# Later tokens' scores of both head halves in one stretch, and low weight parts in operations of 1024 columns, in the mixers of a streaming encoder step

## The chip, the cores and the metric

The kernel runs on 1 core of one Trainium2 chip. The metric is device time in microseconds: 1081.46 us is the median of 3 runs of the kernel before (1081.15 to 1081.49).

## What is computed

One inference step of a two-layer encoder, in float32, for 256 prompt tokens and 32 later tokens ("sample") that also see 512 cached keys and values. A layer is a gated feed-forward block, a mixer, and a second feed-forward block; the mixer is differential attention beside a pooling mixer and a short gated convolution. The part that the change touches is the attention, cut here to its core:

```
q, k, v, u, hc, bg, cg = split(rmsnorm(x) @ w_in)       # D_MODEL 1024 -> 2560
q = rope(q.reshape(b, t, 4, 2, 64)); k = rope(k...)     # 4 heads, 2 halves c of 64
s = einsum('bqhcd,bkhcd->bhcqk', q, k) * 64**-0.5       # later tokens: 512 cached keys + 32 new ones
p = softmax(s)                                          # over keys, for each half
a = p[:, :, 0] - lam * p[:, :, 1]
o = rmsnorm(einsum('bhqk,bkhe->bqhe', a, v), subln)     # into concat(...) @ w_out
```

## The kernel before

The 288 tokens lie along the free dimension, features along the partitions. Every large product is made from two parts of each operand, a rounded high part and the low rest: `mm3` (line 261) issues three TensorE matmuls of 288 columns, wh with xh, wl with xh, wh with xl. Weights come in chunks of 128 x 2048 floats (16 blocks of 128 x 128), loaded by DMA up to three chunks ahead. ACT rounds a chunk to wh, DVE subtracts to get wl. In the feed-forward stages this is done in operations of 1024 columns (lines 108, 109).

In the mixers the order on ACT, DVE and POOL is written by a planner inside the kernel (lines 440 to 560), and so is the place of small work between TensorE's products. Work beside the products is a set of tasks (Python generators). A task runs one step, yields `wait(...)`, and is taken up again when the planner's clock has reached the time at which it is ready: the end of its last step plus LAG = 0.2, and where it needs a PSUM bank, MARGIN = 1.1 more and a free bank. `main` (line 558) issues one triple, moves the clock by 0.369 and polls the tasks. Every step's instructions are charged to their engine with a cost from their length (an ACT copy of 288 columns from PSUM 0.29, of 512 columns from SBUF 0.53; a DVE operation 0.07 + n/960), behind what the planner has already put there. Each engine runs its instructions in the order in which they were issued. In the trace, ACT, DVE and POOL instructions of the mixers all carry line 553, the helper that charges them; they are told apart by tiles.

- `chunk` (line 580) hands out the current chunk; if its split is not complete it issues the rest first, and it starts `split_task` (line 565) for the next chunk. A chunk has two pieces of 8 blocks, a = 0 and 1, and before the change a piece is split in two halves of 4 blocks (SPLIT = 4): wh of a half on ACT, then wl of it on DVE.
- The mixer's chunks 0 to 9 hold w_in, two output tiles each (piece a is tile a, one block per k); chunks 10 to 13 hold w_out. The order of tiles is q0, k0, q1, k1, v0, v1, q2, k2, v2, v3, q3, k3 and then the gates and pools. After a tile, `after` (line 872) starts its task at once: for q and k `rope` (line 611), which begins with four ACT copies of 32 partitions into zw, then z = acc times cosR on DVE, zw times sinR on POOL, and the sum on DVE.
- `attn_p(h)` (line 657) makes the prompt's attention of a head: scores of both halves into the PSUM tile sc, mask and maximum on DVE, exponentials on ACT, transposes and value product through the two tp banks.
- `attn_s` (line 740) makes the later tokens' attention of all four heads at once, head h on partitions 32h to 32h + 31. For each half c in turn it takes sc, multiplies in two column ranges of 272 keys, takes the maximum over 544 and the exponentials. Then the halves are combined, transposed in five blocks, and multiplied with the values in one PSUM tile (line 784).
- `finish_until` (line 942) makes the products with w_out wait for what the tasks deliver; the later tokens' part ("ms") is wanted with the second of four groups.

PSUM has four accumulators, sc of two banks, and two tp banks.

```python
            def ready_at(t):
                _, res, _, dep = t[1]
                at = t[0]
                if dep is not None:
                    at = max(at, done.get(dep, never) + LAG)
                return max(at + MARGIN, min(free[res])) if res else at
```

Of the kernel before, what the change touches and what calls it, by code (L numbers as in the profile page):

```python
# [9 lines left out]
F32 = mybir.dt.float32  # L10
F32R = mybir.dt.float32r
I32 = mybir.dt.int32
AF = mybir.ActivationFunctionType
ALU = mybir.AluOpType
AX = mybir.AxisListType
# [3 lines left out]
P = 128  # L19
D = 1024  # L20
KD = D // P
SEQ = 256
DEC = 32
T = SEQ + DEC
PAST = 512
DEPTH = 2
DFF = 2816
KF = DFF // P
H = 4
HD = 64  # L30
# [34 lines left out]
def tile_step(ctx, tc, xT, head, w_gu, w_dn, w_in, w_out, rest, ck, cvp,  # L65
              yT, kT_o, vT_o, pool_o, conv_o):
    nc = tc.nc
    V, S, G, PE = nc.vector, nc.scalar, nc.gpsimd, nc.tensor

    const = ctx.enter_context(tc.tile_pool(name="const", bufs=1))  # L70
# [3 lines left out]
    tmp = ctx.enter_context(tc.tile_pool(name="tmp", bufs=2))  # L74
    ps_a = ctx.enter_context(tc.tile_pool(name="ps_a", bufs=4, space=PSUM))
    ps_s = ctx.enter_context(tc.tile_pool(name="ps_s", bufs=1, space=PSUM))
    ps_t = ctx.enter_context(tc.tile_pool(name="ps_t", bufs=2, space=PSUM))
# [197 lines left out]
    lam_s = const.tile([P, DEPTH * 2], F32, tag="lam_s", name="lam_s")  # L275

    def lambda_sums():
        lp = const.tile([P, DEPTH * 2, HD], F32, tag="lam_p", name="lam_p")
        la = lam_in.rearrange("o (a b) d -> o a b d", b=2)
        V.tensor_tensor(lp, la[:, :, 0, :], la[:, :, 1, :], ALU.mult)  # L280
        V.tensor_reduce(lam_s, lp, AX.X, ALU.add)
        for l in range(DEPTH):
            li = 0.8 - 0.6 * math.exp(-0.3 * l)
            V.tensor_scalar(gsub[:, l:l + 1], par_t[:, C_SUB + l:C_SUB + l + 1], 1.0 - li, None, ALU.mult)
# [140 lines left out]
    def mixer(l, g_next):  # L425
        with tc.tile_pool(name="mp", bufs=1) as mp, tc.tile_pool(name="mt", bufs=2) as mt, \
                tc.manual_schedule(engines={ET.Activation, ET.DVE, ET.Pool}):
            kts = mp.tile([P, H, PAST + DEC], F32, tag="kts", name="kts")
# [4 lines left out]
            qT = [mp.tile([P, T], F32, tag=f"q{h}", name=f"q{h}") for h in range(H)]  # L433
# [5 lines left out]
            es_t = mp.tile([P, 2, PAST + DEC], F32, tag="es", name="es_t")  # L439
            sms = mp.tile([P, 4], F32, tag="sms", name="sms")  # L440
# [52 lines left out]
            def release(res):  # L493
                slots = free[res]
                slots[slots.index(never)] = stage[1] + LAG
# [34 lines left out]
            def wait(res=None, cost=0.0, dep=None):  # L530
                return (0.0, res, cost, dep)
# [24 lines left out]
            V, S, G = Costed(nc.vector, "dve"), Costed(nc.scalar, "act"), Costed(nc.gpsimd, "pool")  # L556
# [8 lines left out]
            def split_task(i):  # L565
                r3 = raw.pop(i).rearrange("p (a b) -> p a b", b=P)
                whl[i] = []
                pos[1] = i + 1
                for a in range(2):
                    wh = wsp.tile([P, 8, P], F32R, tag="wh", name="wh")  # L570
                    wl = wsp.tile([P, 8, P], F32R, tag="wl", name="wl")
                    whl[i].append((wh, wl))
                    for b in range(0, 8, SPLIT):
                        src, sl = r3[:, 8 * a + b:8 * a + b + SPLIT, :], slice(b, b + SPLIT)
                        yield wait()
                        S.activation(wh[:, sl, :], src, AF.Copy)
                        yield wait()
                        V.tensor_tensor(wl[:, sl, :], src, wh[:, sl, :].bitcast(F32), ALU.subtract)

            def chunk():  # L580
                i = cur[0]
                cur[0] += 1
                load_to(i + 3)
                if i in splits:
                    finish_task(splits.pop(i))
                w = whl.pop(i)
                splits[i + 1] = start(split_task(i + 1))
                return w
# [151 lines left out]
            def attn_s():  # L740
                yield wait(dep=("q", 3))
                yield wait(dep=("k", 3))
                for c in range(2):
                    yield wait("sc", 1.0)
                    sc = ps_s.tile([P, 2, 512], F32, tag="sc", name="scs")
                    r = slice(64 * c, 64 * c + 64)
                    for b in range(2):
                        for h in range(H):
                            PE.matmul(sc[32 * h:32 * h + 32, b, 0:272], qT[h][r, SEQ:T],  # L749
                                      kts[r, h, b * 272:(b + 1) * 272], start=True, stop=True)  # L750
                    yield wait()
                    nm = mt.tile([P, 1], F32, tag="nms", name="nms")
                    V.tensor_reduce(nm, sc[:, :, 0:272], AX.XY, ALU.max)
                    V.tensor_scalar(nm, nm, -0.125, None, ALU.mult)
                    yield wait()
                    S.activation(es_t[:, c, :].rearrange("p (b k) -> p b k", b=2), sc[:, :, 0:272], AF.Exp,
                                 scale=0.125, bias=nm, accum_out=sms[:, c:c + 1])
                    release("sc")
                yield wait()
                fr = mt.tile([P, 1], F32, tag="frs", name="frs")  # L760
                V.reciprocal(fr, sms[:, 1:2])
                V.scalar_tensor_tensor(fr, fr, nlam[:, l:l + 1], sms[:, 0:1], ALU.mult, ALU.mult)
                a = es_t[:, 0, :]
                V.scalar_tensor_tensor(a, es_t[:, 1, :], fr, es_t[:, 0, :], ALU.mult, ALU.add)
                aT = mp.tile([P, 5, P], F32, tag="aTs", name="aTs")
                yield wait("tp", 0.87)
                tp = ps_t.tile([P, 512], F32, tag="tp", name="tps")
                for b in range(4):
                    PE.transpose(tp[:, b * P:(b + 1) * P], a[:, b * P:(b + 1) * P], ident)
                yield wait("tp", 0.22)  # L770
                tp2 = ps_t.tile([P, 512], F32, tag="tp", name="tps2")
                PE.transpose(tp2[:DEC, 0:P], a[:, PAST:], ident)
                S.activation(aT[:, 0:4, :], tp.rearrange("p (b q) -> p b q", b=4), AF.Copy)
                S.activation(aT[:DEC, 4, :], tp2[:DEC, 0:P], AF.Copy)
                release("tp")
                release("tp")
                yield wait(dep="vs")
                yield wait("tp", 1.5)
                o = ps_t.tile([P, 512], F32, tag="tp", name="os")
                for b in range(5):  # L780
                    for h in range(H):
                        kk = slice(0, P) if b < 4 else slice(0, DEC)
                        vv = cvt[:, b, h * P:(h + 1) * P] if b < 4 else vsm[:, h * P:(h + 1) * P]
                        PE.matmul(o[32 * h:32 * h + 32, 0:P], aT[kk, b, 32 * h:32 * h + 32], vv,
                                  start=b == 0, stop=b == 4)
                yield from finish(o, sms[:, 0:1], 1, lambda t: t[:, 0:H, SEQ:T], "ms")
# [130 lines left out]
            for q in range(2):  # L917
                k = KD - 1
# [166 lines left out]
```

## Time and profile before

| | |
|---|---|
| median of 3 runs | 1081.46 us (1081.15 to 1081.49) |
| the profiled execution's own time | 1080.95 us |
| its span in the trace | 1079.2 us |
| first mixer (chunks 0 to 9, then w_out) | about 219.9 to 333 us |
| second mixer | about 749.6 to 862 us |
| TensorE / DVE / ACT busy | 99% / 65% / 49% |

A row of the timeline gives start and length of an instruction or of several alike, then the engine, the line, the operation with what it writes and reads, the shape, the count, and in brackets the idle time before it with what ended it. PE is TensorE. Matmuls are pipelined: one of 288 columns is shown 0.29 us long, while the next begins 0.13 us after it, so a stop of TensorE is read from start to start. A float32 product outside `mm3` appears as two instructions.

### The profile page before, as it was taken

How to read it: one execution, taken by the hardware profiler on the slowest of the kernel's cores; microseconds unless marked ns; L12 is line 12 of the kernel's file. 1: busy time of each engine (PE TensorE's matmuls, PEld its weight loads, DVE VectorE, ACT ScalarE, POOL GpSimd, SP SyncE). 2: the span in 40 equal slices, each digit the busy share in tenths (PEclk: the TensorE clock that was granted, in tenths of full speed). 3: DMA queues.
4: the chain of work that ended last, by engine and by line, in shares of the span. 5: the costliest groups of instructions: out<-in, count | busy, mean ns of one | idle time of the engine just before them, and what ended most of it. 6: DMA issues, size and time to landing. Idle time of an engine off the chain costs nothing.

```text
span 1079.2 us, 19588 instructions
## 1 busy us (share of the span) xinstructions
PE 1066.1 (99%) x8092; PEld 1054.1 (98%) x8092; DVE 698.2 (65%) x1194; ACT 530.4 (49%) x929; POOL 32.7 (3%) x61
## 2 busy tenths in 40 slices
PE   8999999999999999999999999999999999999997
PEld 8999999999999999999999999999999999999997
DVE  5866665547879666655576666554779786666442
ACT  5644444448655444444444444443786644444431
POOL 0000000011200000000000000000112000000000
PEclk9999999999999999999999999999999999999999
DMA  6665444445445544444445444444444364544421
GB/s 242 242 229 180 167 157 160 175 151 179 127 155 208 183 157 159 173 177 157 157 162 184 162 157 169 180 160 176 159 141 158 127 225 174 178 157 159 175 97 44
DMA packets 33257, 180.11 MB, mean 167 GB/s; under 512 B 7696, under 2 KB 10000, under 8 KB 12688
## 3 DMA queue, kind: packets, MB, share of 16 engines
q1 hardware_dynamic: 32880, 178.42, 47.0%
q8 instruction: 63, 1.03, 0.4%
q10 hardware_dynamic: 288, 0.44, 0.1%
q14 instruction: 26, 0.21, 0.1%
HBM read 175.24 MB, written 3.61 MB: 166 GB/s over the span
## 4 chain that ended last, share of the span: by engine, by line
PE 70%; issue 23%; ACT 4%; DVE 2%; DMA 1%; POOLq 0%; SPq 0%; POOL 0%; DVEq 0%; ACTq 0%
PE acc L264 22%; PE acc L266 22%; PE acc L265 22%; ACT zw L553 2%; DMA raw<-in_head 1%; ACT e L553 1%; ACT wh L553 1%; DVE wl L553 0%; PE sc L266 0%; PE sc L264 0%; PE sc L265 0%; PE scs L749 0%; PE sc L663 0%; ACT wh L307 0%; PE acc L314 0%
## 5 line engine op out<-in xcount | busy, mean ns | idle before, releaser
L264 PE MATMUL acc<-xh,wh 128*128 128x288 f32 x1632 | 487.7, 299 | 0.0
L265 PE MATMUL acc<-xh,wl 128*128 128x288 f32 x1632 | 481.1, 295 | 2.4 <-DVE wl L553 2.2
L266 PE MATMUL acc<-xl,wh 128*128 128x288 f32 x1632 | 480.8, 295 | 0.0
L109 DVE TENSOR_TENSOR wl<-raw,wh 128x1024 fp32r<-128x1024 f32 x258 | 315.8, 1225 | 188.2 <-ACT wh L108 188.0
L108 ACT ACTIVATE wh<-raw 128x1024 fp32r<-128x1024 f32 x258 | 273.0, 1060 | 291.6 <-PE acc L266 261.6
L265 PEld LDWEIGHTS acc<-xh,wl 128*128 128x128 f32 x1632 | 308.2, 189 | 4.4 <-DVE wl L553 3.8
L264 PEld LDWEIGHTS acc<-xh,wh 128*128 128x128 f32 x1632 | 307.0, 188 | 2.5 <-issue 1.4
L266 PEld LDWEIGHTS acc<-xl,wh 128*128 128x128 f32 x1632 | 307.4, 188 | 0.0
L264 PE MATMUL acc<-hh,wh 128*128 128x288 f32 x704 | 208.6, 296 | 0.0
L265 PE MATMUL acc<-hh,wl 128*128 128x288 f32 x704 | 208.0, 295 | 0.0
L266 PE MATMUL acc<-hl,wh 128*128 128x288 f32 x704 | 207.3, 294 | 0.0
L266 PEld LDWEIGHTS acc<-hl,wh 128*128 128x128 f32 x704 | 132.8, 189 | 0.0
L265 PEld LDWEIGHTS acc<-hh,wl 128*128 128x128 f32 x704 | 132.2, 188 | 0.0
L264 PEld LDWEIGHTS acc<-hh,wh 128*128 128x128 f32 x704 | 132.0, 188 | 0.0
L370 ACT ACTIVATE hh<-t 128x288 fp32r<-128x288 f32 x88 | 39.0, 444 | 108.0 <-DVE t L369 108.0
L553 DVE TENSOR_TENSOR wl<-raw,wh 128x512 fp32r<-128x512 f32 x112 | 77.0, 703 | 6.0 <-ACT wh L553 5.4
L553 ACT ACTIVATE wh<-raw 128x512 fp32r<-128x512 f32 x112 | 65.7, 627 | 6.6 <-PE acc L266 4.1
L371 DVE TENSOR_TENSOR hl<-t,hh 128x288 fp32r<-128x288 f32 x88 | 40.2, 458 | 39.1 <-ACT hh L370 38.8
L364 DVE TENSOR_TENSOR t<-acc,R 128x288 f32<-128x288 f32 x82 | 37.5, 457 | 31.6 <-PE acc L266 31.3
L367 ACT ACTIVATE t<-t 128x288 f32<-128x288 f32 x88 | 37.7, 429 | 6.7 <-DVE t L364 6.3
L369 DVE TENSOR_TENSOR t<-t,t 128x288 f32<-128x288 f32 x88 | 39.6, 451 | 0.0
L418 DVE SCALAR_TENSOR_TENSOR xall<-acc,xall 128x288 f32<-128x288 f32 x32 | 14.6, 456 | 37.0 <-PE acc L266 36.8
(196 smaller groups left out, 808.9 us busy)
## 6 DMA issues: line engine op xcount, KB each, us to landing
raw<-in_w_gu SPq DMA_DIRECT2D x85, 1024.0 KB, 4.8
raw<-in_w_dn SPq DMA_DIRECT2D x44, 1024.0 KB, 4.8
raw<-in_w_in SPq DMA_DIRECT2D x20, 1024.0 KB, 4.9
raw<-in_w_out SPq DMA_DIRECT2D x8, 1024.0 KB, 5.0
raw<-in_head SPq DMA_DIRECT2D x7, 528.0 KB, 6.8
kts<-in_ck SPq DMA_DIRECT2D x2, 1024.0 KB, 5.2
cvt<-in_cv SPq DMA_DIRECT2D x2, 1024.0 KB, 7.0
xall<-in_xT SPq DMA_DIRECT2D x1, 1152.0 KB, 9.6
```

The source lines that it names most:

```text
L108: S.activation(wh, src, AF.Copy)
L109: V.tensor_tensor(wl, src, wh.bitcast(F32), ALU.subtract)
L264: PE.matmul(acc, wh[:, b, :], mh, start=first, stop=False)
L265: PE.matmul(acc, wl[:, b, :], mh, start=False, stop=False)
L266: PE.matmul(acc, wh[:, b, :], ml, start=False, stop=last)
L364: V.tensor_tensor(t1, ag[:, :T], R, ALU.mult)
L367: S.activation(t1, t1, AF.Silu)
L369: V.tensor_tensor(h, t1, t2, ALU.mult)
L370: S.activation(hh[j], h, AF.Copy)
L371: V.tensor_tensor(hl[j], h, hh[j].bitcast(F32), ALU.subtract)
L418: V.scalar_tensor_tensor(xs[m], acc[:, :T], 0.5, xs[m], ALU.mult, ALU.add)
L553: return f(out, *a, **kw)
```

## The change

The later tokens' scores of both halves are made in one stretch: sixteen products in the order key range, head, half, the 32 new keys of each half into one of the two tp banks and the 512 cached keys into one bank of sc. The new keys' scores are copied to SBUF by ACT, the maximum is taken over both parts, and there are two exponentials per half, whose sums are added. In the mixers' splits, wh is still rounded in two halves, and wl of a piece is then written by one operation over all eight blocks. A small scratch tile of the lambda sums moves to a buffer that the first feed-forward stage uses.

```diff
@@ lambda_sums
-        lp = const.tile([P, DEPTH * 2, HD], F32, tag="lam_p", name="lam_p")
+        lp = tmp.tile([P, T], F32, tag="t1", name="lam_p")[:, 0:DEPTH * 2 * HD].rearrange("p (a d) -> p a d", d=HD)
@@ split_task, for each of the two pieces a
                     for b in range(0, 8, SPLIT):
                         src, sl = r3[:, 8 * a + b:8 * a + b + SPLIT, :], slice(b, b + SPLIT)
                         yield wait()
                         S.activation(wh[:, sl, :], src, AF.Copy)
-                        yield wait()
-                        V.tensor_tensor(wl[:, sl, :], src, wh[:, sl, :].bitcast(F32), ALU.subtract)
+                    yield wait()
+                    V.tensor_tensor(wl, r3[:, 8 * a:8 * a + 8, :], wh.bitcast(F32), ALU.subtract)
@@ attn_s
-                for c in range(2):
-                    yield wait("sc", 1.0)
-                    sc = ps_s.tile([P, 2, 512], F32, tag="sc", name="scs")
-                    r = slice(64 * c, 64 * c + 64)
-                    for b in range(2):
-                        for h in range(H):
-                            PE.matmul(sc[32 * h:32 * h + 32, b, 0:272], qT[h][r, SEQ:T],
-                                      kts[r, h, b * 272:(b + 1) * 272], start=True, stop=True)
-                    yield wait()
-                    nm = mt.tile([P, 1], F32, tag="nms", name="nms")
-                    V.tensor_reduce(nm, sc[:, :, 0:272], AX.XY, ALU.max)
-                    V.tensor_scalar(nm, nm, -0.125, None, ALU.mult)
-                    yield wait()
-                    S.activation(es_t[:, c, :].rearrange("p (b k) -> p b k", b=2), sc[:, :, 0:272], AF.Exp,
-                                 scale=0.125, bias=nm, accum_out=sms[:, c:c + 1])
-                    release("sc")
-                yield wait()
+                yield wait("sc")
+                yield wait("tp")
+                yield wait("tp", 1.3)
+                tn = [ps_t.tile([P, 512], F32, tag="tp", name="scn") for _ in range(2)]
+                sc = ps_s.tile([P, 2, 512], F32, tag="sc", name="scs")
+                for dst, k0, n in ((tn, PAST, DEC), ([sc[:, 0, :], sc[:, 1, :]], 0, PAST)):
+                    for h in range(H):
+                        for c in range(2):
+                            r = slice(64 * c, 64 * c + 64)
+                            PE.matmul(dst[c][32 * h:32 * h + 32, 0:n], qT[h][r, SEQ:T], kts[r, h, k0:k0 + n],
+                                      start=True, stop=True)
+                yield wait()
+                sn = mt.tile([P, 2, DEC], F32, tag="sn", name="sn", bufs=1)
+                for c in range(2):
+                    S.activation(sn[:, c, :], tn[c][:, 0:DEC], AF.Copy)
+                    release("tp")
+                nm = mt.tile([P, 4], F32, tag="nms", name="nms")
+                V.tensor_reduce(nm[:, 0:2], sc, AX.X, ALU.max)
+                V.tensor_reduce(nm[:, 2:4], sn, AX.X, ALU.max)
+                V.tensor_tensor(nm[:, 0:2], nm[:, 0:2], nm[:, 2:4], ALU.max)
+                V.tensor_scalar(nm[:, 0:2], nm[:, 0:2], -0.125, None, ALU.mult)
+                yield wait()
+                for c in range(2):
+                    S.activation(es_t[:, c, 0:PAST], sc[:, c, :], AF.Exp, scale=0.125, bias=nm[:, c:c + 1],
+                                 accum_out=sms[:, c:c + 1])
+                release("sc")
+                for c in range(2):
+                    S.activation(es_t[:, c, PAST:], sn[:, c, :], AF.Exp, scale=0.125, bias=nm[:, c:c + 1],
+                                 accum_out=sms[:, 2 + c:3 + c])
+                yield wait()
+                V.tensor_tensor(sms[:, 0:2], sms[:, 0:2], sms[:, 2:4], ALU.add)
```

## Rows read from the trace of the kernel before

**Rows 1.** The profile's page, part 1: busy time of each engine, its share of the span and its instructions.
```profile
span 1079.2 us, 19588 instructions
...
PE 1066.1 (99%) x8092; PEld 1054.1 (98%) x8092; DVE 698.2 (65%) x1194; ACT 530.4 (49%) x929; POOL 32.7 (3%) x61
```

**Rows 2.** Busy time of each engine in one stretch, the first mixer: the stretch and its length in us, busy us (instructions) of PE, PEld, DVE, ACT and POOL, the granted TensorE clock as a share of full speed, the busy share of the DMA engines and GB/s.
```profile
219.90:303.70 83.80, 81.76 (x657) 76.78 (x656) 63.31 (x166) 56.49 (x160) 15.12 (x26) 1.00 0.46 153
```

**Rows 3.** For whom TensorE waited, first two lines in the first mixer (215 to 345 us), last two in the second (745 to 870 us): us in total, times, longest us.
```profile
PE acc L265 <- DVE wl L553: 1.6, 3, 1.1
PE sc L663 <- ACT e L553: 0.3, 1, 0.3
...
PE sc L663 <- ACT e L553: 0.7, 1, 0.7
PE acc L265 <- DVE wl L553: 0.6, 1, 0.6
```

**Rows 4.** TensorE in order of time around the first score stretch of the later tokens in the first layer (start us, length in us of the row, instruction, shape, count). The rows of the stretch are each a look at one instant, so that the instructions in flight at that instant stand in one row.
```profile
279.21 0.29 PE L266 MATMUL acc<-xl,wh 128*128 128x288 f32 x1
...
279.44 0.43 PE L749 MATMUL scs<-kts,q 64*32 64x272 f32 x4
...
279.92 0.41 PE L749 MATMUL scs<-kts,q 64*32 64x272 f32 x4
...
280.15 0.41 PE L749 MATMUL scs<-kts,q 64*32 64x272 f32 x4
...
280.49 0.41 PE L264 MATMUL acc<-xh,wh 128*128 128x288 f32 x1
280.74 0.29 PE L265 MATMUL acc<-xh,wl 128*128 128x288 f32 x1
```

**Rows 5.** TensorE around the prompt's scores of one head in the second layer, same columns.
```profile
803.00 0.71 PE L663 MATMUL sc<-k,q 64*128 64x256 f32 x4
803.53 0.40 PE L664 MATMUL sc<-k,q 64*128 64x128 f32 x4
803.86 0.40 PE L264 MATMUL acc<-xh,wh 128*128 128x288 f32 x1
```

**Rows 6.** TensorE in the value product of the later tokens, first layer: the instructions over the last 32 keys, in flight at two instants.
```profile
297.10 0.31 PE L784 MATMUL os<-vsm,aTs 32*32 32x128 f32 x4
...
297.24 0.29 PE L784 MATMUL os<-vsm,aTs 32*32 32x128 f32 x4
```

**Rows 7.** The tile scs by instruction: count, shortest/median/longest ns, first and last start in us, shapes.
```profile
L553 DVE TENSOR_REDUCE nms<-scs x4: 715/718/719, 281.4 to 815.1; 128x1 f32<-128x544 f32 x4
L553 ACT ACTIVATE es_t<-scs,nms x4: 713/716/718, 282.4 to 816.1; 128x544 f32<-128x544 f32 x4
```

**Rows 8.** DVE's last operation on the later tokens' part of ml in the first layer, and the product with which the second group of w_out begins.
```profile
303.56 0.35 DVE L553 SCALAR_TENSOR_TENSOR ml<-tpo,gsub,mh 128x128 fp32r<-128x128 f32 x1
...
306.94 0.30 PE L264 MATMUL acc<-mh,wh 128*128 128x288 f32 x1
```

**Rows 9.** DVE's instructions grouped by line and shape: count, busy us, mean ns of one, idle time before them and what ended it. L109 stands in the feed-forward stages, L553 in the mixers.
```profile
L109 DVE TENSOR_TENSOR wl<-raw,wh 128x1024 fp32r<-128x1024 f32 x258 | 315.8, 1225 | 188.2 <-ACT wh L108 188.0
L553 DVE TENSOR_TENSOR wl<-raw,wh 128x512 fp32r<-128x512 f32 x112 | 77.0, 703 | 6.0 <-ACT wh L553 5.4 <-issue 0.3
```

**Rows 10.** ACT, DVE and TensorE in order of time in the first mixer, around the start of chunk 2.
```profile
232.32 0.62 ACT L553 ACTIVATE wh<-raw 128x512 fp32r<-128x512 f32 x1
234.36 1.65 ACT L553 ACTIVATE zw<-acc 32x288 f32<-32x288 f32 x4 [1.42 <-DVE q L553]
236.03 0.63 ACT L553 ACTIVATE wh<-raw 128x512 fp32r<-128x512 f32 x1
...
234.55 0.68 DVE L553 TENSOR_TENSOR wl<-raw,wh 128x512 fp32r<-128x512 f32 x1
...
236.70 0.73 DVE L553 TENSOR_TENSOR wl<-raw,wh 128x512 fp32r<-128x512 f32 x1 [0.20 <-ACT wh L553]
...
235.29 0.40 PE L265 MATMUL acc<-xh,wl 128*128 128x288 f32 x1 [1.07 <-DVE wl L553]
235.53 0.30 PE L266 MATMUL acc<-xl,wh 128*128 128x288 f32 x1
```

**Rows 11.** The same engines in the second mixer, around the start of chunk 2.
```profile
761.86 0.63 ACT L553 ACTIVATE wh<-raw 128x512 fp32r<-128x512 f32 x1
762.52 1.65 ACT L553 ACTIVATE zw<-acc 32x288 f32<-32x288 f32 x4
764.19 0.63 ACT L553 ACTIVATE wh<-raw 128x512 fp32r<-128x512 f32 x1
...
764.86 0.74 DVE L553 TENSOR_TENSOR wl<-raw,wh 128x512 fp32r<-128x512 f32 x1 [0.20 <-ACT wh L553]
...
763.56 0.29 PE L265 MATMUL acc<-xh,wl 128*128 128x288 f32 x1
```

**Rows 12.** TensorE at the start of chunk 2's second tile, first mixer and second.
```profile
239.52 0.29 PE L264 MATMUL acc<-xh,wh 128*128 128x288 f32 x1
239.89 0.40 PE L265 MATMUL acc<-xh,wl 128*128 128x288 f32 x1
...
767.66 0.29 PE L264 MATMUL acc<-xh,wh 128*128 128x288 f32 x1
768.03 0.40 PE L265 MATMUL acc<-xh,wl 128*128 128x288 f32 x1
```

## The prediction

> **What bounds the kernel now.** I read the page first: TensorE is busy for 1066.1 of 1079.2 us with 8092 matmuls, one every 0.13 us, while DVE is busy for 65% [rows 1]. So time goes only where that beat is broken. The windows show that the mixer of one layer leaves TensorE idle for 83.80 - 81.76 = 2.0 us and that its clock is granted in full, 2.4 GHz [rows 2]; the rest of a broken beat is small work between the products. The waits then say on what TensorE stands in the mixers: in the first on low weight parts of DVE (three waits, 1.6 us) and on the scores' bank held by ACT (0.3 us), in the second on both too (0.6 and 0.7 us) [rows 3]. The change touches both kinds of loss: the later tokens' score stretch, and the operations that write the low parts.
>
> Durations come from the profiled execution: 1080.95 us, of which the trace spans 1079.2; it stands 0.5 us below the median of 1081.46 us, and I add the sum to the median. About 0.2% (2.2 us) is what a measurement of this kernel can tell from no change.
>
> **Part 1, the scores.** Before, each layer has two stretches of 16 instructions (8 products of 272 columns, two passes each). In the first, four instructions run side by side on the four column strips; the first group of four starts at 279.44, the third at 279.92 and the fourth at 280.15, so 0.23 to 0.24 us each, and the next products follow at 280.49 and 280.74 [rows 4]. From the product before (279.21) to 280.74 are 1.53 us; two beats of 0.13 off leave 1.27. Of these 4 x 0.23 = 0.92 stream, 0.34 is fixed (entering, loading, leaving). The second stretch has the same instructions; two cost 2.5 us per layer.
>
> After, one stretch holds eight strips at once (two row halves, four column strips), because c runs innermost and each half has its own bank. Do row halves really overlap? Head by head, the prompt's scores put two halves in one stretch: x4 start at 803.00, the next x4 at 803.53, the next product at 803.86 [rows 5]. That is 0.86 us for work that takes 8 passes; one after the other, at the 0.23 us per 272 columns of [rows 4], four passes of 256 and four of 128 columns would need 4 x 0.22 + 4 x 0.11 = 1.3. So halves overlap, and I take eight strips as side by side. The past: two groups of 512 columns, 0.23 x 512/272 = 0.43 each, 0.86. The new keys: two groups of 32 columns; the nearest row, short groups with loads of 32 columns, shows 0.14 between groups (297.10, 297.24) [rows 6], so 0.28. With 0.34 fixed: 1.48 per layer instead of 2.5. **Gain 1.0 per layer, 2.0 in all.** Bounds: if the short groups cost nothing, 2.6; if halves don't overlap, four groups of 0.43 and four of 0.14 with 0.34 give 2.6, a loss of 0.2 over both layers.
>
> The Trainium skill, TensorE: Matmul & The Clock Gate (Part 3, Measured speedup vs the span model), speaks against the full gain: packed tiles reach less than their number there, 3 tiles 2.38x and 9 tiles 6.32x. As an estimate from that page, eight tiles would gain some 5.6x, the two long groups would take 1.2 us, and the change would give 1.3 us instead of 2.0. No row shows eight strips. Two row halves at full width show no such loss: side by side they need 2 x 0.22 + 2 x 0.11 = 0.66, and the 0.86 us of [rows 5] leave only 0.2 for entering. So I stay with the rows.
>
> DVE and ACT in this part: two reductions of 0.715 us and two exponentials of 0.716 us [rows 7] become one reduction over 1024 columns (by length about 1.3 us), a small one, four exponentials and two copies. I estimate 0.1 us more on DVE and 1.2 more on ACT per layer. I cost this at nothing: the attention of the later tokens reaches its last low part at 303.56 + 0.35 = 303.91, and TensorE wants it with the second group of w_out at 306.94 [rows 8], 3.0 us later; a chain up to 3 us longer stays covered. The stretch now holds sc and both tp banks. The planner asks for sc, then tp, then tp, each 1.3 us of its clock after the last; what is queued behind are head 3's transposes and its value product, which want a tp bank. They come back two copies after the scores; if ACT is inside a 0.63 us rounding then, TensorE stands up to 0.5 us per layer (bounds 0 and 0.5; I take 0.1 each).
>
> **Part 2, the low parts.** Two operations of 703 ns become one of 1225 ns [rows 9]: DVE saves 0.18 us, 56 times, about 10 us in all. That gain I cost at nothing, DVE having a third of its time free. What counts is when the first low part of a tile is there. Before, TensorE starts on blocks 0 to 3; after, it needs all eight rounded first, one more ACT operation, and 1225 ns. Mostly that is covered, since a chunk is split one chunk (over 6 us) ahead. It is not at **chunk 2 of each mixer**, where the rotary copies fill ACT.
>
> First mixer: ACT rounds blocks 0-3 at 232.32, then runs the four zw copies of tile 1 from 234.36, and only then rounds blocks 4-7 at 236.03; DVE writes the first low part at 234.55, the second at 236.70, and TensorE goes on at 235.29 [rows 10]. Will the second rounding stay behind those copies? By the planner's own costs yes: eight zw copies and R (0.29 each) lie ahead of the first rounding, whose end it puts past 10 us from the mixer's start, while tile 1's copies are issued at 8.9, when its products end (24 triples of 0.369); the second rounding is ready only after that. And z is ready sooner than a low part that waits for it. So the wide operation starts where the second short one did, 236.70, and ends 1.225 + 0.05 (POOL's zw beside it stretches it so, 0.73 against 0.68) later, 237.98; TensorE goes on 0.06 later, at 238.03. **A loss of 2.74.** Second mixer: same order, ACT at 761.86, 762.52, 764.19, second low part at 764.86, TensorE unhindered at 763.56 [rows 11]. After: 764.86 + 1.28 + 0.06 = 766.20, **a loss of 2.64**.
>
> How much comes back? TensorE arrives late at each later wait, and those waits shrink. For tile 2 of the chunk it stood from 239.52 to 239.89 and from 767.66 to 768.03, 0.24 each beyond the beat [rows 12]. In [rows 3], idle time counts from the end of a product that lasts 0.29, so a wait costs 0.16 more than shown: first mixer 0.5 idle in two further waits, 0.8; the scores' bank 0.3. Second: 0.8 and 0.7. The last of them, in chunk 4, goes for a second reason: a split passes DVE's queue twice instead of four times, so its last part is planned earlier. After a wait the next beat is 0.1 longer (235.29 to 235.53, [rows 10]); five such pairs fall away. Returned: 0.24 + 0.8 + 0.3 + 0.24 + 0.8 + 0.7 + 0.5 = 3.6. Net of part 2: 2.74 + 2.64 - 3.6 = **+1.8**. Bounds: all 5.4 lost if nothing comes back; -0.8 if the second rounding moves ahead of the copies. What is late next is chunk 6: tile 7's copies may again sit before a rounding; I take 0.1 per layer.
>
> **Part 3, lam_p** in a t1 buffer: one operation in the first gate/up stage, where DVE idles 188 us waiting for ACT [rows 9]. Nothing; without that cover its cost would be one small operation.
>
> **Sum:** -2.0 + 1.8 + 0.2 + 0.2 = +0.2 us, that is 1081.6 us, no change that can be told.
>
> **Rivals.** *Nothing comes back (slower).* Place: chunk 2 of both mixers. It decides if DVE and ACT, which work on what TensorE made, are late by as much as TensorE, so that every later wait stays. For it: zw copies and exponentials follow TensorE's tiles. Against: the scores' bank is held by exponentials of tiles made before chunk 2. Price 5.4 instead of 1.8: 1085.2 us; half of it, 1083.4. Chance 0.18. *The second rounding goes ahead of the copies (faster).* Then the wide part starts on DVE about when the first short one did, costs half a microsecond to 0.8 at chunk 2, all of it returned, and the later waits go as well: part 2 gives -0.8 and the sum 1078.7 us. For it: the plan asks for it right after the first. Against: the order of ACT in both mixers. Chance 0.13. *The eight strips don't run as eight (the change doesn't do what it says):* part 1 gives +0.2 instead of -2.0, 1083.8 us. Against: [rows 4, 5]. Chance 0.07.
>
> **How the numbers follow.** The forecast has 0.62. The range goes from just above the faster rival's time, 1079.1, to 1084.4, which takes in the third rival and half of the first; about 0.18 is left out. Faster by over 0.2%: nearly all of the second rival, 0.02 of the forecast's spread: 0.15. Slower: most of the first, half of the third, 0.02 of the spread: 0.23. Within: 0.62.
>
> **What would show it.** Right: one score stretch per layer of about 1.5 us with starts in eights; TensorE stopped for over 2.5 us on a wide wl at chunk 2 of both mixers; no wait on the scores' bank; chunk 4's wait gone. Wrong: ACT rounding twice in a row ahead of tile 1's copies at chunk 2; starts still in fours; waits at chunk 3 or 4 as long as before; a stop at head 3's value product.

## The result and the profile after

The changed kernel took **1096.09 us** (median of 4 runs, 1094.09 to 1096.35) against 1081.47 us before: ratio 1.0128, 95% interval [1.0116, 1.0141]. That is 14.6 us slower; the prediction had 1081.6 us, at most 1084.4. The profiled execution took 1096.06 us. One run of e1 (2677.76 us) and one of e8 (1475.26 us) are far off the others and stand in no median or ratio below.

The page's part 1 after, beside [rows 1]: TensorE has 3 us more in its rows and 15 us more span, DVE 54 instructions fewer and 2.4 us less work.

```profile
span 1094.3 us, 19558 instructions
...
PE 1069.1 (98%) x8092; PEld 1055.8 (96%) x8092; DVE 695.8 (64%) x1140; ACT 532.8 (49%) x941; POOL 37.4 (3%) x61
```

The first mixer between the same two products as in [rows 2]: 7.3 us longer, 8.0 instead of 2.0 us idle, and a mean granted clock of 0.96.

```profile
221.97:313.04 91.07, 83.10 (x656) 77.73 (x655) 62.91 (x147) 57.20 (x164) 16.99 (x26) 0.96 0.45 142
```

For whom TensorE waited in the first mixer (first five lines) and in the second, beside [rows 3]. The scores' bank is gone, and of the low parts one wait per mixer is left, a long one. Four waits are new, on the tiles ml, vcat, es_t and aTs. (acc are the large products; tps the transposes of the later tokens' combined exponentials es_t, and aTs their copy in SBUF; tpo the transposes of an attention output, read into mh and ml; tpv and tpvs those of the values, vcat the later tokens' values; pd and yp the pooling mixer's input and product.)

```profile
PE acc L265 <- DVE wl L553: 3.8, 1, 3.8
PE tps L786 <- ACT aTs L553: 1.8, 1, 1.8
PE tps L783 <- DVE es_t L553: 1.3, 1, 1.3
PE tpv L640 <- DVE ml L553: 0.6, 1, 0.6
PE tpvs L650 <- DVE vcat L553: 0.4, 1, 0.4
...
PE acc L265 <- DVE wl L553: 2.5, 1, 2.5
PE tps L786 <- ACT aTs L553: 1.8, 1, 1.8
PE tps L783 <- DVE es_t L553: 1.3, 1, 1.3
PE tpv L640 <- DVE ml L553: 0.6, 1, 0.6
PE tpvs L650 <- DVE vcat L553: 0.4, 1, 0.4
```

**Where the time went.** TensorE issues the same number of products into acc in both kernels, so the start of the n-th (counted from 0) can be compared. Before the first mixer, at n = 1387 (200.03 us before), the changed kernel is 2.07 us behind, all from start-up. At n = 2693 (400.1), after the first mixer, it is 9.86 behind, at n = 6221 (900.0), after the second, 15.10. So the mixers cost **7.8 and 5.2 us**, 13.0 in all. The start-up's part is not put down to the change: at the same product, executions of the kernels below stand between 0.5 us before and 2.7 us behind, whatever their mixers hold. In the three that are furthest behind (this one, e6 and e7, 1.95 to 2.67 us) the granted clock of the first 35 us is 0.95, in all others 1.00. The growth of the mixers leaves the start-up out.

**Chunk 2 of the first mixer**, beside [rows 10]: ACT, DVE and TensorE in order of time, first mixer.

```profile
234.40 0.62 ACT L553 ACTIVATE wh<-raw 128x512 fp32r<-128x512 f32 x1
236.44 1.64 ACT L553 ACTIVATE zw<-acc 32x288 f32<-32x288 f32 x4 [1.42 <-DVE q L553]
238.10 0.63 ACT L553 ACTIVATE wh<-raw 128x512 fp32r<-128x512 f32 x1
...
238.77 1.27 DVE L553 TENSOR_TENSOR wl<-raw,wh 128x1024 fp32r<-128x1024 f32 x1 [0.20 <-ACT wh L553]
...
240.09 0.61 PE L265 MATMUL acc<-xh,wl 128*128 128x288 f32 x1 [3.79 <-DVE wl L553]
240.49 0.44 PE L266 MATMUL acc<-xl,wh 128*128 128x288 f32 x1
```

The copies stay ahead of the second rounding, and TensorE goes on at 240.09, 238.02 on the clock of before. The two products after the stop stand 0.40 us apart, not 0.24. The windows over this place say why: the granted clock is 0.50 (1.2 GHz) from 240 to 245 us, after TensorE had been busy for 1.30 of 5 us.

```profile
235.00:240.00 5.00, 1.30 (x9) 0.92 (x7) 3.79 (x11) 3.46 (x9) 0.95 (x2) 0.85 0.10 30
240.00:243.00 3.00, 2.91 (x11) 2.66 (x11) 2.49 (x6) 2.60 (x5) 0.80 (x1) 0.50 0.11 38
243.00:245.00 2.00, 2.00 (x10) 1.59 (x10) 0.20 (x2) 0.00 (x0) 0.00 (x0) 0.50 0.53 120
245.00:250.00 5.00, 5.00 (x38) 5.00 (x38) 3.02 (x8) 3.28 (x11) 0.00 (x0) 0.97 0.54 203
```

The second mixer's stop (beside [rows 11]) ends at 776.04, after 2.46 us of idle time, and the clock stays at 1.00 there.

**The score stretch**, beside [rows 4]: TensorE, first layer; the middle row is a look at one instant.

```profile
291.52 0.29 PE L266 MATMUL acc<-xl,wh 128*128 128x288 f32 x1
...
291.83 1.07 PE L752 MATMUL scs<-kts,q 64*32 64x512 f32 x16
...
292.83 0.40 PE L264 MATMUL acc<-xh,wh 128*128 128x288 f32 x1
293.06 0.29 PE L265 MATMUL acc<-xh,wl 128*128 128x288 f32 x1
```

The sixteen past products start in two groups of eight, at 291.83 and at 292.26, 0.43 us apart: eight strips do run side by side. From 291.52 to 293.06 less two beats, the stretch costs 1.28 us and is the only one.

**The later tokens' transposes.** Before, es_t was complete 1.0 us ahead of the first four of the five transposes, and these cost TensorE 0.44 us beyond the beat, without a wait (DVE and TensorE, first layer):

```profile
289.68 0.79 DVE L553 SCALAR_TENSOR_TENSOR es_t<-es_t,frs 128x544 f32<-128x544 f32 x1
...
291.50 0.60 PE L769 MATMUL tps<-ident,es_t 128*128 128x128 f32 x4
```

After, DVE in order of time between the scores' end and the five transposes, first layer, and TensorE and ACT at the transposes:

```profile
293.40 1.22 DVE L553 TENSOR_TENSOR wl<-raw,wh 128x1024 fp32r<-128x1024 f32 x1
294.54 0.45 DVE L553 TENSOR_TENSOR cgR<-acc,R 128x288 f32<-128x288 f32 x1
295.02 0.53 DVE L553 TENSOR_TENSOR cext<-cgR,hcR 128x256 f32<-128x256 f32 x2
295.47 1.22 DVE L553 TENSOR_REDUCE nms<-scs 128x2 f32<-128x1024 f32 x1
...
297.19 1.22 DVE L553 TENSOR_TENSOR wl<-raw,wh 128x1024 fp32r<-128x1024 f32 x1
298.32 1.07 DVE L553 SCALAR_TENSOR_TENSOR cy<-cext,rest,cy 128x290 f32<-128x290 f32 x2
...
301.23 1.32 DVE L553 SCALAR_TENSOR_TENSOR es_t<-es_t,frs 128x544 f32<-128x544 f32 x1
302.47 1.72 DVE L553 TENSOR_TENSOR wl<-raw,wh 128x1024 fp32r<-128x1024 f32 x1
304.12 0.44 DVE L553 TENSOR_TENSOR cgR<-acc,R 128x288 f32<-128x288 f32 x1
304.59 0.53 DVE L553 TENSOR_TENSOR cext<-cgR,hcR 128x256 f32<-128x256 f32 x2
...
302.69 0.63 PE L783 MATMUL tps<-ident,es_t 128*128 128x128 f32 x4 [1.29 <-DVE es_t L553]
308.14 0.28 PE L786 MATMUL tps<-ident,es_t 128*32 128x128 f32 x1 [1.83 <-ACT aTs L553]
...
305.66 0.54 ACT L553 ACTIVATE cy<-cext,rest 128x290 f32<-128x290 f32 x1 [3.71 <-DVE ws L553]
306.10 0.46 ACT L553 ACTIVATE mh<-tpo,gsub 128x256 fp32r<-128x256 f32 x1
306.46 1.14 ACT L553 ACTIVATE wh<-raw 128x512 fp32r<-128x512 f32 x2
307.50 0.58 ACT L553 ACTIVATE aTs<-tps 128x512 f32<-128x512 f32 x1
```

The reduction nms, whose input is ready at 292.9, starts at 295.47 behind a wide low part and the gate's products; es_t ends at 302.55, behind a second wide part and the convolution's cy. Two of the chain's own operations are longer too than in e1 below, frs 0.57 us (0.22 there) and es_t 1.32 (0.79). The fifth transpose waits for a copy on ACT that stands behind cy. The trace puts the wait of cy down to DVE's ws; this and the cext that cy reads stand behind a third wide part of 1.72 us.

### The profile page after: what moved, and what is told of

It is laid out like the page before. It is cut to its first block, busy times and chain, and to the rows that moved or that the text cites. A ratio compares the mean times of both kernels' runs of the same rounds, so it can differ in the third digit from the quotient of the medians.

```text
span 1094.3 us, 19558 instructions
## 1 busy us (share of the span) xinstructions
PE 1069.1 (98%) x8092; PEld 1055.8 (96%) x8092; DVE 695.8 (64%) x1140; ACT 532.8 (49%) x941; POOL 37.4 (3%) x61
## 4 chain that ended last, share of the span: by engine, by line
PE 64%; issue 23%; DVE 5%; ACT 5%; POOL 1%; DMA 1%; POOLq 0%; SPq 0%; DVEq 0%; ACTq 0%
PE acc L264 20%; PE acc L266 20%; PE acc L265 20%; ACT zw L553 2%; DVE wl L553 1%; PE acc L314 1%; ACT e L553 1%; ACT wh L553 1%; DVE nm L553 1%; DMA raw<-in_head 1%; ACT on L553 1%; PE sc L314 1%; PE sc L266 0%; PE sc L264 0%; PE sc L265 0%
## 5 line engine op out<-in xcount | busy, mean ns | idle before, releaser
L109 DVE TENSOR_TENSOR wl<-raw,wh 128x1024 fp32r<-128x1024 f32 x258 | 315.7, 1224 | 188.4 <-ACT wh L108 188.1
L553 DVE TENSOR_TENSOR wl<-raw,wh 128x1024 fp32r<-128x1024 f32 x56 | 69.2, 1238 | 10.2 <-ACT wh L553 10.2
L553 ACT ACTIVATE wh<-raw 128x512 fp32r<-128x512 f32 x112 | 64.9, 625 | 6.8 <-PE acc L266 4.4
L264 PE MATMUL acc<-mh,wh 128*128 128x288 f32 x128 | 38.2, 299 | 0.1
```

The source lines that it names most:

```text
L109: V.tensor_tensor(wl, src, wh.bitcast(F32), ALU.subtract)
L264: PE.matmul(acc, wh[:, b, :], mh, start=first, stop=False)
L553: return f(out, *a, **kw)
```

## The experiments

Each is compared with the kernel before on the same chip. The growth of a mixer is worked out as above (n = 1387, 2693 and 6221 of the profiled execution, start-up left out):

```
kernel               median us   ratio to before, 95%      first mixer  second
after                 1096.09    1.0128 [1.0116, 1.0141]     +7.79      +5.24
e1_scores_only        1081.63    1.0001 [0.9992, 1.0011]     +0.25       0.00
e2_wide_only          1091.78    1.0091 [1.0075, 1.0107]     +5.62      +5.22
e3_pair_first         1097.96    1.0147 [1.0131, 1.0163]     +6.92      +9.37
e4_rounds_together    1087.97    1.0060 [1.0042, 1.0078]     +4.53      +2.95
e5_fill_stop          1094.68    1.0121 [1.0107, 1.0135]     +5.59      +6.81
e6_wide_early         1091.74    1.0102 [1.0086, 1.0117]     +6.05      +5.04
e7_wide_late          1081.80    1.0000 [0.9991, 1.0009]     -0.29      -0.22
e8_scores_later       1082.99    1.0018 [1.0008, 1.0028]     +0.86      +0.58
e9_late_pool          1080.49    0.9990 [0.9981, 0.9998]     -0.40      -0.33
e10_rounds_early      1081.28    0.9995 [0.9986, 1.0003]     +0.62      -0.57
e11_both              1081.47    1.0000 [0.9992, 1.0009]     +0.47      -0.76
e12_all_but_two       1084.73    1.0041 [1.0027, 1.0055]     +1.81      +1.55
```

**e1: the scores alone** (the mixers' low parts as before; lam_p stays in its new buffer, where it shows no cost).

> The score stretch alone; low parts in halves again. Theory W+S (the wide low parts cause the stops at chunk 2, the new score chain causes the two stops at the later tokens' transposes): chunk 2 as before the change (1.3 us stop in the first mixer, full clock), the two stops at the transposes stay (some 3.9 us per layer), the stretch saves 1.2 us per layer: 1081.5 + 2 x (3.9 - 1.2) = 1086.9 us. Rival (wide operations ahead of it on DVE make the score chain late): no stops at the transposes, 1081.5 - 2.4 = 1079.1 us.

```
-                    V.tensor_tensor(wl, r3[:, 8 * a:8 * a + 8, :], ...)
+                        V.tensor_tensor(wl[:, sl, :], src, ...)
```

No change in time. The score stretch is as in the kernel after (1.29 us in place of two), so it saves 1.2 us per layer; and it is given back. New is a wait of the pool's last product on pd, 0.7 us per layer; the transposes tps and tpo take another 0.6. So the stretch's gain is real and worth nothing by itself, and the stops at tps are not the scores' doing alone.

**e2: the wide low parts alone** (the scores and lam_p as before).

> The wide low parts alone; scores in two stretches as before the change. Theory W+S: stops of 4.2 and 2.6 us at chunk 2, half clock after the first, no wait on the scores' bank at chunk 3, some 1.2 us of new waits in the chunks after it, no stops at the later tokens' transposes: 1081.5 + (4.7 - 0.9 + 1.4) + (2.4 - 0.9 + 1.1) = 1089.3 us. Rival: stops at the transposes here too, 3.9 us per layer more, 1097 us.

```
-                sc = ps_s.tile([P, 2, 512], F32, tag="sc", name="scs")
-                for dst, k0, n in ((tn, PAST, DEC), ...
+                for c in range(2):
+                    yield wait("sc", 1.0)
+                    ... two stretches, as before
```

10.3 us slower. Chunk 2's stop is there in both mixers (3.8 and 2.5 us idle), here with a slow clock after both (0.71 in the window 240 to 245 us, 0.70 from 773 to 777), and so are the waits on ml and vcat; nothing waits at tps. So the wide parts alone lose 10.8 us in the mixers, where both changes together lose 13.0, and yet **the stops at tps, 3.1 us idle per mixer, stand in neither half of the change** and come with both. (In their place e2 has waits on pd, 0.7 us per mixer, and the slow clock in its second mixer.)

**e3: both transposes' banks taken first.**

```
-                yield wait("tp", 0.87)
+                yield wait("tp")
+                yield wait("tp", 1.09)
                 ... four transposes
-                yield wait("tp", 0.22)
                 ... fifth transpose
```

> The changed kernel, in which the later tokens' attention takes both tp banks before its five transposes, so that no other task's transposes come between the fourth and the fifth. If the second stop (2.0 us per layer) comes from head 3's transposes slipping in between: it goes, the first stop (1.6) stays, 1096.1 - 4 = 1092 us. Rival (the chain is late whatever the banks): the first stop grows by what the second loses, 1096 us.

Neither holds as worded: the two stops become one of 2.8 us per mixer, "PE tps L786 <- DVE ml". The four transposes, 21 products into acc later now, no longer wait: es_t ends at 299.99, they start at 302.06. The fifth waits for the other tp bank, which holds an attention output until DVE's ml has read it, and ml (304.96) stands behind two more wide parts. So work on DVE is late by about as much whichever piece TensorE asks for first. The second mixer grows by 9.4 us, more than in the kernel after: its stops are followed by a slow clock, at chunk 2 (0.73 from 773 to 777 us) and here (0.50 from 840 to 843).

**e4: both roundings of a tile in one step** (wide everywhere).

```
+                    yield wait()
                     for b in range(0, 8, SPLIT):
-                        yield wait()
                         S.activation(wh[:, sl, :], src, AF.Copy)
                     yield wait()
                     V.tensor_tensor(wl, ...)
```

> The changed kernel with both roundings of a piece in one step, the second right behind the first and ahead of the zw copies of tile 1. If the copies between the two roundings set the stop at chunk 2: the wide part begins ahead of z, the stop falls from 4.1 to some 2.4 us in the first mixer, with the clock at full speed (2.1 us more), and from 2.6 to some 1.3 in the second: 1096.1 - 1.7 - 2.1 - 1.3 = 1091 us. Rival (DVE's queue or the raw chunk's arrival sets it): stops as long as before, 1096 us.

The mixers grow by 7.5 us instead of 13.0. The copies do go behind both roundings, the stop at chunk 2 shrinks from 3.8 to 2.2 us idle in the first mixer and to 0.8 in the second, and the stops at tps give way to others (1.1 us per mixer at tpo, 0.9 at tpa). More is gained than the stop itself: what comes later in the mixer hangs on chunk 2. The full clock that was expected in the first mixer did not come: after the stop of 2.2 us it is 0.50 from 238 to 240 us.

**e5: TensorE kept busy during the stop** of the first mixer. Seven products that nobody reads, ahead of chunk 2:

```
+                if l == 0 and i == 4:
+                    for n in (4, 3):
+                        idle = ps_t.tile([P, 512], F32, tag="tp", name="idle")
+                        for _ in range(n):
+                            PE.matmul(idle[:, :T], ones, xs[0], start=True, stop=True)
```

> The kernel after, with seven idle matmuls (the ones matrix by the first tile of x, 288 columns each, into two tp banks that nobody reads) ahead of chunk 2 of the first mixer, so that TensorE isn't idle while it waits for that chunk's low part. Theory: the 5 us at a granted clock of 0.50 that follow this stop (240 to 245 us in the kernel after) come from TensorE having stood idle for 3.8 us. Then chunk 2 starts no earlier, about 240.1 us, but the granted clock of the next 5 us is 0.9 or more and the time falls by 2.1 to 2.6 us, to about 1093.8 us. Rival: the clock falls for another reason (its turn comes at that moment, whatever stands there); then the clock is 0.50 there or somewhat later as before, and the time is 1096.1 us.

The granted clock after the stop, the same stretches as above:

```profile
235.00:240.00 5.00, 4.38 (x22) 3.41 (x21) 3.76 (x8) 4.45 (x11) 1.30 (x2) 1.00 0.10 30
240.00:243.00 3.00, 3.00 (x24) 2.68 (x24) 2.50 (x7) 1.59 (x4) 0.32 (x1) 1.00 0.19 55
243.00:245.00 2.00, 2.00 (x18) 2.00 (x17) 1.97 (x5) 1.18 (x7) 0.00 (x0) 1.00 0.92 258
...
773.00:777.00 4.00, 4.00 (x22) 3.33 (x22) 2.57 (x8) 2.29 (x5) 0.82 (x1) 0.63 0.35 64
```

1.00 where it was 0.50, and the first mixer grows 2.2 us less: here the slow clock followed from TensorE standing idle. In the same execution the second mixer's stop, which was not filled, is followed by a clock of 0.63 and 1.6 us more growth, so the median falls by 1.4 us only. The stops at tps stay as they were (1.3 and 1.8 us).

**e6, e7, e12: which chunks are wide.** In e6 those below 7 of each mixer, in e7 those from 7 on, in e12 all but chunk 2; the others in halves as before, the scores in one stretch.

```
-                        yield wait()
-                        V.tensor_tensor(wl[:, sl, :], src, ...)
+                        if not wide:
+                            yield wait()
+                            V.tensor_tensor(wl[:, sl, :], src, ...)
+                    if wide:
+                        yield wait()
+                        V.tensor_tensor(wl, r3[:, 8 * a:8 * a + 8, :], ...)
     wide = i - first_chunk < 7        # e6
     wide = i - first_chunk >= 7       # e7
     wide = i - first_chunk != 2       # e12
```

> The kernel after, with wide low parts in chunks 0 to 6 of each mixer alone, and halves (512 columns) from chunk 7 on. Theory E: the stops at the later tokens' transposes near the end of each mixer (3.9 us per mixer) come from wide operations standing beside that chain on VectorE; then they go, while the stop at chunk 2 and the small stops in the middle stay: 1096.1 less 7 to 8, about 1088.5 us. Theory L: the end is late because the planner's order was already thrown back by the stop at chunk 2; then the stops at the end stay and the time is about 1096 us.

> The kernel after, with halves in chunks 0 to 6 of each mixer and wide low parts from chunk 7 on alone. Theory E (the stops at the end come from wide operations beside the chain): they stay, the stop at chunk 2 and its slow clock go: 1082.3 us (the scores' change alone) and 7 to 8, about 1089.5 us. Theory L (the end is late from what was lost at chunk 2): no stop is left, about 1082.5 us.

> The kernel after with halves in chunk 2 of each mixer alone, wide low parts in all other chunks. The stop at chunk 2 and the slow clock behind it (5.4 us in the first mixer, 2.7 in the second, in the kernel after) should go under either theory. Theory A: the stops at the end, for which wide parts early and late were both needed, come from what the stop at chunk 2 left late; then they go as well (another 7 to 8 us) and the time is about 1081 to 1083 us. Theory B: they come from the order that the planner forms with the wide parts of chunks 3 to 6; then they stay, with the small stops in the middle (1.4 and 1.1 us): 1096.1 less 8, about 1088 us.

Neither E nor L of the first two holds. The stops at tps are gone in e6 **and** in e7: wide parts late in the mixer cost nothing by themselves (e7 is level with before), wide parts early cost what e2 showed (11.1 us for both mixers in e6, 10.8 in e2; in e6 a wait on pd of 1.0 us per mixer and a slow clock after the second stop, 0.70, stand in for the stops at tps), and only together do they make those stops. e12 then finds the place: **halves in chunk 2 alone take back 9.7 of the 13.0 us**, the stop beyond the 1.1 us of before, the slow clock (1.00 from 235 to 245 us), the waits at tpv and tpvs and the wait on es_t, though wide parts stand beside the scores as in the kernel after. It keeps 3.4 us: TensorE waits 1.0 us per mixer for vsm and 1.1 at the fifth transpose. So theory A holds in the main, but not in its wording. Not the time lost matters, since the stops at tps are 1.3 and 1.8 us alike after a loss at chunk 2 of 4.9 us (first mixer, with the slow clock), 2.6 (second) and 2.75 (e5). What differs is DVE's order. From the first score product to the end of es_t there pass 10.8 us in after, e3 and e5, and 7.5 to 7.7 in e1, e6, e7, e9 and e12; between the scores' end and the end of es_t DVE works 9.4 us in the former, 5.5 to 5.9 in the latter. e4, wide everywhere and without a stop at tps, stands between (9.1 and 7.7 us), so it is not the width of chunk 2's parts by itself. The planner sets that order by its own clock, from what it has issued up to then. By which of its decisions chunk 2's wide parts turn it, was not tried, and stays open.

**e8: two steps later** (the scores alone, as e1).

```
-                yield wait("tp", 0.87)
+                yield (1.0, "tp", 0.87, None)     # the four transposes
-                yield wait("tp", 0.48)
+                yield (1.2, "tp", 0.48, None)     # the pool's product
```

> The scores' change alone, halves in the mixers, with two steps of TensorE's order put later: the transposes of the later tokens' first half by 1.0 us and the pool's last product by 1.2 us of the planner's time. Theory: the score stretch saves 1.2 us per layer, and what took it back are short waits at just these steps (0.7 us at the pool's product, 0.2 each at the transposes), so the waits shrink: 1082.3 less 1.2 to 2.4 (the waits of both layers), about 1080.3 us. Rival: the waits only move to what follows (the output product, the last transposes): 1081.5 to 1082.5 us.

The rival, and somewhat worse: the wait on pd is gone, and the fifth transpose waits 1.9 us per layer for ml instead (ratio 1.0018, where e1 has 1.0001).

**e9, e10, e11: better than both?** All as e7; e9 moves the second pool product alone, e10 puts both roundings of chunk 2 in one step, with its two short low parts behind them, e11 does both.

```
-                yield wait("tp", 0.48)
+                yield (1.2 if g == 1 else 0.0, "tp", 0.48, None)     # e9, e11
```

```
+                    together = i - first_chunk == 2                  # e10, e11
                     for sl in parts:
-                        yield wait()
+                        if not together or sl is parts[0]:
+                            yield wait()
                         S.activation(wh[:, sl, :], src[:, sl, :], AF.Copy)
```

> Halves in chunks 0 to 6, wide low parts from chunk 7 on (the kernel of the run before that stood at 1081.8 us), with one step later: the second pool product of each mixer is put 1.2 us later in the planner's time, which moves it behind the forty short matmuls of the later tokens' output and changes nothing else in TensorE's order but one transpose. Theory: the score stretch's 1.2 us per layer are eaten by waits near the end, of which this product's (0.8 to 0.9 us per layer) is the largest; with it behind the forty matmuls, pd is ready: 1081.8 less 1.6 to 1.8, about 1080.1 us. Rival: the wait moves to the forty matmuls or to the output product, 1081.3 to 1082 us.

> Halves in chunks 0 to 6, wide low parts from chunk 7 on, and in chunk 2 alone both roundings of a tile in one step ahead of the query's four copies on ScalarE. Theory: the kernel before waits 1.5 us (1.1 in one piece) at chunk 2 of the first mixer for the low part of its second half, because that half's rounding stands behind the copies; with the roundings together this wait goes: 1081.8 less 1.1 to 1.5, about 1080.6 us. Rival: the copies that come 0.6 us later make the first score late by as much, and the order of the planner shifts: 1081.8 us or some more.

> Both: the second pool product later, and both roundings of chunk 2 in one step. If the two theories hold, 1081.8 less 2.7 to 3.3, about 1078.8 us; if both waits only move, 1081.5 to 1082 us.

e9 is faster than the kernel before by 0.9 us, ratio 0.999 [0.9981, 0.9998], the only one of thirteen whose interval lies below 1, and only just; its mixers account for 0.7 of it. (The rest goes with the clock: 7 of the 28 runs of before that it is held against show a mean granted clock below 0.998, none of its own eleven.) Of that e7 has 0.5 already: the wait on pd (0.8 us per mixer) is gone in e9, but tpo waits 0.6 for ACT in its place, which is the rival's course. In e10 the wait at chunk 2 did not go but grew from 1.1 to 1.7 us in the first mixer, and what it gains in the second it loses there. Its expectation had the wrong half: in e7 TensorE goes on at 237.24, when DVE's first low part (236.50, 0.68 us) is done, and in e10 that part stands behind the key's sums on DVE as well (234.35 to 234.87). The longer wait is also followed by a slow clock, 0.51 from 237 to 240.5 us, where e7 has 1.00. The four runs of e10 with a mean granted clock of 0.999 have a median of 1079.27 us, the seven at 0.996 or 0.997 one of 1081.60. e11 keeps that wait and that slow clock and is level with before.

## Why the prediction was wrong

- **The score stretch was right**, and a little better: 1.28 us in place of two of 1.27 [rows 4], a gain of 1.26 per layer where 1.0 was forecast. The rows' rate was right, 0.43 us per group of 512 columns. The Trainium skill's page TensorE: Matmul & The Clock Gate (Part 3, Measured speedup vs the span model) let an estimate of 1.3 us in all stand against it; the two groups of eight start 0.43 us apart, without such a loss, and the measurement decides.
- **Chunk 2's stop was right** in place, cause and size: 238.02 forecast as 238.03 in the first mixer, and in the second 2.62 us late at its first low product (776.04 - 763.56 - 9.86) where 2.64 was forecast.
- **The waits that were to shrink did go** (the scores' bank, the later low parts; [rows 3] against the waits above). Yet of the 3.6 us returned nothing is left over: the slow clock took 2.2 of it in the first mixer (e5), and two waits that were not foreseen (on ml and vcat) stand in the middle, 1.0 us idle per mixer. The wide parts alone cost 10.8 us (e2) where +1.8 was forecast and 5.4 was the bound. The prediction priced the stop at chunk 2 by its own length alone; the trace of before had none so long in a mixer, and no bound was put on what follows one.
- **The step that failed** is "I cost this at nothing ... a chain up to 3 us longer stays covered". It is the largest part of the miss: 6.2 us of idle time where the term was nothing, of the 12.8 us by which the mixers missed the sum (13.0 against 0.2); the slow clock is 2.2, the waits on ml and vcat 2.0, and the rest was not followed up. The chain was held against the wrong deadline: w_out's second group, which is the last to want it (there it was 3.0 us early before; after, the last low part ends at 316.93, and the group starts at 316.60, some 0.2 us off the beat). The chain's own transposes stand in TensorE's order long before, at places that the planner fixed, and TensorE waits there: 1.3 and 1.8 us idle per mixer. At the first of them the chain had 1.0 us in hand before, not 3.0. And from the first score product to the end of es_t it takes no longer than before (11.0 us then, 10.8 now), but TensorE's order leaves it less: 54 products into acc from the first score product to the first transpose, where there were 60 and two score stretches.
- **What kept the chain from getting shorter**, as it does with the scores' change alone (7.5 us in e1, with 42 products to the first transpose), was not its own work, as the prediction had weighed (0.1 us on DVE, 1.2 on ACT), but what stood ahead of it on DVE. Alone, neither part of the change does that (e1, e2). "DVE having a third of its time free" is an average, and says nothing of a queue in which DVE works 8.1 us from the scores' end before it starts the one operation that TensorE waits for (4.8 in e1).
- **The rivals**: 1085.2 us, with nothing coming back, was nearest in time and still 11 us off; its mechanism is not what happened, since the later waits did go. No rival let the two parts act on each other, which made the stops at tps (e1, e2), nor gave chunk 2 a say in the order at the mixer's end (e12). All four signs of being right were there, and none of the wrong ones: no sign looked at the chain or at the clock.

## What to carry to other kernels

A longer operation on an engine with free time is not free where it delays the first piece that another engine waits for: keep the short pieces there (one chunk of fourteen per mixer here). Wide ones elsewhere do less harm, but in this kernel they gained nothing that can be told (e7 against e1). Hold a longer chain against the first place in the waiting engine's order that needs it, not the last. Where a planner orders the work, an edit early in a stage changes the order of everything behind it, so two edits are costed together or tried together.

## What the runs showed of the hardware

- A stop of TensorE of 3.8 us idle was followed by 5 us at 1.2 GHz, and cost 2.2 us more. Shorter stops were followed by a slow clock in some executions and not in others: those of 2.5 us in e2, e3, e5 and e6 (0.70, 0.73, 0.63 and 0.70 from 773 to 777 us) but not in the kernel after, one of 2.2 us in e4 (0.50 from 238 to 240), one of 1.7 us in e10 (0.51 from 237 to 240.5) and e11, but not those of 1.8 us at the fifth transpose in the kernel after. None followed the stops of 1.1 us in before, e1, e7, e8, e9 and e12. What decides between them no run here shows.
- DVE and POOL took longer where they worked side by side: the wide low part at 302.47 took 1.72 us where 1.22 is usual, es_t 1.32 where e1 has 0.79, and POOL's copies into cext, two columns, rose from a mean of 182 to 664 ns.

```profile
302.05 1.06 POOL L553 TENSOR_TENSOR ws<-ws 128x311 f32<-128x311 f32 x1
303.05 0.10 POOL L553 MEMSET cext<- 128x2 f32 x1
303.09 1.14 POOL L553 COPY cext<-rest 128x2 f32<-128x2 f32 x1
```

The Trainium skill gives a reason, on SBUF — State Buffer (Who interferes with whom): GpSimd's ports are VectorE's second pair, held as an exclusive lock. The trace agrees: POOL's copy of two columns ends with the wide part beside it (304.23 and 304.19).
